# Padding the 264-column slots so that every working tile starts at the same 256-byte phase

## The chip, the cores and the metric

The kernel runs on one core of one Trainium2 chip. The metric is the device time of one execution in microseconds (us). The core has five engines that work at the same time: TensorE (PE; its weight loads are listed as PEld), VectorE (DVE), ScalarE (ACT), GpSimd (POOL) and SyncE (SP, which here issues the transfers). They share an on-chip memory of 128 partitions, SBUF; matmul results go to PSUM, eight banks of 128 x 512 float32. An address in SBUF means the same byte offset in each partition.

## The reference

One decoder layer on 1024 tokens of width 1024, in float32: half a feed-forward block, two attention branches side by side, another half feed-forward block, and a gated per-layer input.

```python
def swiglu(h, w_gate, w_up, w_down):
    return (jax.nn.silu(h @ w_gate) * (h @ w_up)) @ w_down

x = x + 0.5 * swiglu(rms_norm(x, ffn1_norm), ffn1_w_gate, ffn1_w_up, ffn1_w_down)   # D_FF = 2816
h = rms_norm(x, mix_norm)
fq, fk, fv, f_logit, sq, sk, sv, g_fox, g_sb = split_columns(h @ w_in)
# 8 + 8 heads of 64: forgetting attention (causal softmax with cumulated log gates)
# and stick-breaking attention (strictly causal)
merged = sigmoid(g_fox) * (y_fox @ w_branch_fox) + sigmoid(g_sb) * (y_sb @ w_branch_sb)
x = x + merged @ w_out
x = x + 0.5 * swiglu(rms_norm(x, ffn2_norm), ffn2_w_gate, ffn2_w_up, ffn2_w_down)
x = x + sigmoid(rms_norm(x, ple_norm) @ w_ple_gate) * (p @ w_ple_proj)
```

## The kernel before

**Precision.** Each float32 operand of a matmul is split into a high part in fp32r and a low part, the rest (`split` at L102: ACT copies at L103, DVE subtracts at L104; for plain weights ACT at L127 and POOL at L137). A product takes three passes: high by high, high by low, low by high.

**Feed-forward.** Gate and up projections go block by block (256 columns of the weight), each 2x2 block product in seven products instead of eight, from sums of blocks. `product` (L460 to L471, the matmul at L469) runs one of the seven: a group of 12 matmuls, three passes over four 128-row pieces, with a 128x128 stationary piece of the weight tile and a 128x512 moving piece of the tokens' tile. The first blocks go the plain way through L424. The down projection (L364) runs the same scheme with tiles `H` on both sides. A hand-written table (`seqn`) sets the order; the weight tile of a group is prepared four groups ahead (`LA = 4`). POOL makes the sums of weight blocks (L437 to L442).

**Where the weight tiles lie.** The pool `sb` has 13 kinds of slots (tags), each with a fixed number of buffers that are used in turn (`BUFS`). In the feed-forward blocks the prepared weight tile goes, after the first twelve, to a fixed cycle of tags:

```python
tag = tags["hl"][k] if k < len(tags["hl"]) else ("WL", "WL", "WL", "Q", "Q", "PT")[k % 6]
```

`WL` has three buffers and `Q` two, so one round of six groups goes through WL slots 0, 1, 2, Q slots 0, 1 and a PT slot. The moving tiles of L469 lie in `H`, `X` and `T`.

**Middle.** The mixing projections run with tokens stationary (`nat_steps`, L696, 256 or 264 columns moving) or weights stationary (`feat_steps`, L704, 512 tokens moving, weights in `WH` and `WL`); attention runs scores (L935, L936, moving tiles `KH` and `KL`), transposes (L987) and the product with the values (L1009), and the L704 work that is left is put between these in small pieces. The branch projections are L1210 (stationary `WH`, `WL`, moving `H`), the last stage L1477 (stationary `H`, moving `WH`, `WL`, `T`, `GF`, `RN`, `PT`). L854 is the projection of the per-layer input, L224 transposes.

**Slots.** A slot of a tag is as large as the largest tile that the tag ever holds. Three kinds hold tiles of 4 x 264 columns in the mixing projections (the 8 forget logits ride along with 256 columns): `WH`, `WL` and `Y`, so their slots have 4224 bytes, 16.5 times 256. All others are multiples of 256. Tiles lie one behind the other in each partition in the order of first use: X, PT, H, T, WH, KH, KL, WL, Y, Q, GF, RN, RAW. `slot` (L56) asks the pool for a tile, and everything named above is allocated by it.

Of the kernel before, what the change touches and what calls it, by code (L numbers as in the profile page):

```python
# [18 lines left out]
P = 128  # L19
# [10 lines left out]
PSUM = {"sc": 3, "pt": 2, "av": 1, "pf": 2}  # L30
BUFS = {"X": 2, "H": 4, "RAW": 2, "WH": 3, "WL": 3, "T": 4, "GF": 2, "RN": 2,
        "Q": 2, "KH": 2, "KL": 2, "Y": 2, "PT": 3}
FQ, FK, FV, FL, SQ, SK, SV, GFOX, GSB = 0, 512, 1024, 1536, 1544, 2056, 2568, 3080, 4104


@with_exitstack
def tile_hybrid_decoder_layer(
# [6 lines left out]
    nc = tc.nc  # L44
    cp = ctx.enter_context(tc.tile_pool(name="const", bufs=1))
    st = ctx.enter_context(tc.tile_pool(name="stats", bufs=4))
    sb = ctx.enter_context(tc.tile_pool(name="sb", bufs=2))
# [4 lines left out]
    def nm(s):  # L52
        uid[0] += 1
        return f"{s}_{uid[0]}"

    def slot(tag, shape, dt=F32):  # L56
        return sb.tile(shape, dt, tag=tag, bufs=BUFS[tag], name=nm(tag))

    def stat(shape, tag, bufs=4):
        return st.tile(shape, F32, tag=tag, bufs=bufs, name=nm(tag))  # L60
# [51 lines left out]
    def wraw_load(pieces, nk, n, tag="RAW"):  # L112
        raw = slot(tag, [P, nk, n])
        c = 0
        for src in pieces:
            w = src.shape[-1]
            nc.sync.dma_start(raw[:, :, c:c + w], src)
            c += w
        return raw
# [5 lines left out]
    def whigh(raw, nk, n, tag):  # L125
        hi = slot(tag, [P, nk, n], F32R)
        order("wh", nc.scalar.copy(hi[:], raw[:]))  # L127
        return hi

    def wlow(raw, hi, nk, n, tag, eng_lo=nc.gpsimd):  # L130
        lo = slot(tag, [P, nk, n], F32R)
        if nk == 1:
            parts = [(slice(None), slice(None), slice(i * n // 2, (i + 1) * n // 2)) for i in range(2)]
        else:
            parts = [(slice(None), slice(i * nk // 2, (i + 1) * nk // 2)) for i in range(2)]
        for part in parts:
            ins = eng_lo.tensor_sub(lo[part], raw[part], f(hi[part]))  # L137
            if eng_lo is nc.gpsimd:
                order("wl", ins)
        return lo  # L140
# [900 lines left out]
    def mix_start():  # L1041

        mx["v"], mx["qk"] = {}, {}
        mx["u1"] = v_units(FV + 256, NH, mx["v"])
        tags = (("T", "GF"), ("T", "Y"))
        mx["u2"] = fox_qk_units(FOX_PAIRS[0], mx["qk"], tags, "KH")
        q0 = FOX_PAIRS[0] * P
        pieces = [[kp(win)[:, 4 * kh:4 * kh + 4, a:a + n] for a, n in cols] for cols in (((FV + 256, 256 + NH),), ((FQ + q0, P), (FK + q0, P))) for kh in range(2)]
        raws = {}

        def load_v(X):
            raws["v"] = [wraw_load(pieces[kh], 4, 256 + NH, "Y") for kh in range(2)]

        def split_v(X):
            mx["v"]["w"] = [wsplit(raws["v"][kh], 4, 256 + NH, NAT[kh]) for kh in range(2)]

        def load_qk(X):
            raws["qk"] = [wraw_load(pieces[2 + kh], 4, 256) for kh in range(2)]

        def end(X, N):  # L1060
            hT.extend(halves(N))
            store_x(X, 1)
            for cell in loads[:2]:
                cell[1] = None
            side = posts(N[1], (24, 64, 104, 144), lambda: bank("pt"))
            side[48] = [lambda: mx["qk"].update(w=[wsplit(raws["qk"][kh], 4, 256, tags[kh]) for kh in range(2)])]
            weave(seq(*[g for _, g in mx["u1"][:4] + mx["u2"][:4]]), side)
        return {3: [load_v], 4: [split_v], 5: [lambda X: store_x(X, 0)], 6: [load_qk], "end": end}
# [164 lines left out]
    X = [slot("X", [P, 4, D]) for _ in range(2)]  # L1233
# [86 lines left out]
    X, N = ffn(N, ffn1_w_gate, ffn1_w_up, ffn1_w_down, mix_norm[0], x[0], ad[0], tags, first_entry, mix_start())  # L1320
# [178 lines left out]
    X, hT = [], []  # L1499
# [34 lines left out]
```

## Time and profile before

| What | Value |
|---|---|
| runs | 2302.49, 2301.84, 2300.70 us; median 2301.84 |
| the profiled execution, first to last instruction (span) | 2300.6 us |
| busy PE / DVE / ACT / POOL | 2269.6 / 1468.0 / 980.7 / 829.9 us |
| PE clock granted, mean | 0.999 |
| moved by DMA | 275.49 MB, mean 120 GB/s |
| first feed-forward: products, then down | about 60 to 450, then 450 to 655 us |
| mixing, attention, branches, output | about 655 to 1580 us |
| second feed-forward: products, then down | about 1580 to 1990, then 1990 to 2195 us |
| last stage | about 2195 to 2300 us |

The profiled execution's own time is known as its span; the median of the three runs stands 1.2 us above it. In the rows below, `ps<-H,WL` names the tiles of an instruction without their numbers, `x1008` is how many there are, and `L469` the line of the kernel before. Matmuls overlap in the pipeline, so the mean length of one (some 390 ns) is more than the distance from one start to the next.

### The profile page before, as it was taken

The numbers are of one execution on the slowest core, as the hardware profiler recorded it, in microseconds if no ns is written. First come the engines' busy times: TensorE is split into PE (matmuls) and PEld (weight loads), VectorE is DVE, ScalarE is ACT, GpSimd is POOL, SyncE is SP. The second block draws the span as 40 slices with busy tenths as digits, with TensorE's granted clock in tenths as the row PEclk, the third lists the DMA queues.
The fourth block names the chain that finished last, engine by engine and source line by source line (L and its number), as shares of the span: only waits on it lengthen the run. The fifth ranks groups of instructions, "written<-read, shape, count | busy, mean of one in ns | idle before, by whom it ended". The sixth has DMA issues, their size and how long they took to land.

```text
span 2300.6 us, 30661 instructions
## 1 busy us (share of the span) xinstructions
PE 2269.6 (99%) x11466; PEld 1913.6 (83%) x11466; DVE 1468.0 (64%) x2199; ACT 980.7 (43%) x1742; POOL 829.9 (36%) x762
## 2 busy tenths in 40 slices
PE   9999999999999999899999999999999999999999
PEld 6888888888888999798988778888888888888887
DVE  8855555588863566456656766789645454778753
ACT  6433333333442555555555554246333333334431
POOL 2344444300033556545455645400534343200111
PEclk9999999999999999999999999999999999999999
DMA  3232323484332122422133235732423232655232
GB/s 138 92 124 83 124 83 123 142 307 168 103 120 75 52 79 74 137 79 71 50 82 89 74 115 199 258 139 74 138 78 128 78 128 78 226 213 205 70 106 92
DMA packets 188279, 275.49 MB, mean 120 GB/s; under 512 B 27097, under 2 KB 110297, under 8 KB 188130
## 3 DMA queue, kind: packets, MB, share of 16 engines
q1 hardware_dynamic: 188128, 273.53, 35.4%
q8 instruction: 90, 1.47, 0.3%
q14 instruction: 59, 0.48, 0.1%
q10 hardware_dynamic: 2, 0.00, 0.0%
HBM read 189.83 MB, written 75.27 MB: 115 GB/s over the span
## 4 chain that ended last, share of the span: by engine, by line
PE 55%; DVE 2%; ACT 1%; issue 0%; DVEq 0%; ACTq 0%
PE ps L469 18%; PE ps L364 12%; PE ps L704 9%; PE ps L1477 4%; PE ps L1210 4%; PE ps L1009 2%; PE ps L696 2%; PE ps L987 2%; DVE RN L911 1%; PE ps L424 1%; PE ps L936 1%; PE ps L935 1%; PE ps L854 1%; PE ps L224 0%; DVE H L104 0%
## 5 line engine op out<-in xcount | busy, mean ns | idle before, releaser
L364 PE MATMUL ps<-H,H 128*128 128x512 f32 x2184 | 497.8, 389 | 1.2 <-DVE X L372 1.2
L364 PEld LDWEIGHTS ps<-H,H 128*128 128x128 f32 x2184 | 409.3, 188 | 86.8 <-issue 2.0
L469 PE MATMUL ps<-H,WL 128*128 128x512 f32 x1008 | 244.6, 394 | 0.6 <-ACT WL L103 0.6
L469 PEld LDWEIGHTS ps<-H,WL 128*128 128x128 f32 x1008 | 189.7, 188 | 44.7 <-ACT WL L103 1.0
L704 PE MATMUL ps<-H,WH 128*128 128x512 f32 x768 | 209.5, 401 | 2.1 <-DVE PT L819 2.1
L137 POOL TENSOR_TENSOR WL<-RAW,WH 128x512 fp32r<-128x512 f32 (+1 forms) x108 | 129.4, 1219 | 101.2 <-ACT WH L127 72.9
L704 PEld LDWEIGHTS ps<-H,WH 128*128 128x128 f32 x768 | 136.8, 188 | 26.3 <-DVE PT L819 3.0
L990 DVE TENSOR_TENSOR PT<-ps,PT 128x512 fp32r<-128x512 f32 (+1 forms) x160 | 101.2, 633 | 84.4 <-ACT PT L989 83.6
L137 POOL TENSOR_TENSOR WL<-Y,WH 128x512 fp32r<-128x512 f32 (+1 forms) x10 | 14.4, 1465 | 383.1 <-ACT WH L127 383.1
L469 PE MATMUL ps<-H,Q 128*128 128x512 f32 x600 | 143.9, 390 | 0.0
L372 DVE SCALAR_TENSOR_TENSOR X<-ps,X 128x512 f32<-128x512 f32 x168 | 109.0, 685 | 50.9 <-PE ps L364 50.9
L696 PE MATMUL ps<-WH,H 128*128 128x256 f32 (+1 forms) x896 | 131.7, 286 | 2.0 <-ACT RN L753 0.7
L469 PEld LDWEIGHTS ps<-H,Q 128*128 128x128 f32 x600 | 112.6, 188 | 24.5
L989 ACT CAST PT<-ps 128x512 fp32r<-128x512 f32 (+1 forms) x160 | 87.2, 547 | 106.7 <-PE ps L987 102.1
L469 PE MATMUL ps<-X,WL 128*128 128x512 f32 x504 | 123.8, 394 | 0.0
L696 PEld LDWEIGHTS ps<-WH,H 128*128 128x128 f32 x896 | 116.5, 189 | 4.1 <-ACT RN L753 0.9
L469 PEld LDWEIGHTS ps<-X,WL 128*128 128x128 f32 x504 | 94.9, 188 | 22.0
L1009 PE MATMUL ps<-PT,X 128*128 128x256 f32 (+1 forms) x640 | 104.4, 283 | 8.8 <-DVE PT L990 8.8
L1009 PEld LDWEIGHTS ps<-PT,X 128*128 128x128 f32 x640 | 94.7, 190 | 21.0 <-DVE PT L990 11.0
L704 PE MATMUL ps<-H,WL 128*128 128x512 f32 x384 | 108.6, 404 | 0.0
L948 POOL TENSOR_TENSOR T<-T,l 128x128 f32<-128x128 f32 (+3 forms) x64 | 73.3, 1149 | 89.6 <-DVE l L947 87.2
L911 DVE TENSOR_TENSOR_SCAN RN<-GF,RN 128x127 f32<-128x127 f32 (+2 forms) x96 | 102.2, 1065 | 2.7
(400 smaller groups left out, 4680.0 us busy)
## 6 DMA issues: line engine op xcount, KB each, us to landing
hidden<-PT SPq DMA_DIRECT2D x40, 512.0 KB, 3.1
WH<-in_ffn_w_gate_dram SPq DMA_DIRECT2D x38, 512.0 KB, 5.0
Q<-hidden SPq DMA_DIRECT2D x24, 512.0 KB, 6.4
hidden<-RN SPq DMA_DIRECT2D x22, 512.0 KB, 2.6
RAW<-in_w_in_dram SPq DMA_DIRECT2D x22, 512.0 KB, 4.1
KH<-in_ffn_w_up_dram SPq DMA_DIRECT2D x20, 512.0 KB, 5.8
KL<-in_ffn_w_up_dram SPq DMA_DIRECT2D x20, 512.0 KB, 6.6
T<-in_ffn_w_down_dram SPq DMA_DIRECT2D x20, 512.0 KB, 4.4
```

The costliest lines, as they stand in the source:

```text
L137: ins = eng_lo.tensor_sub(lo[part], raw[part], f(hi[part]))
L364: pe(nc.tensor.matmul(groups[g][t][:], act[:, a, k, t * P:(t + 1) * P], wt[:, b, k, :], start=(fresh and n == 0), stop=(i in (6, 1, 4) and ...
L372: nc.vector.scalar_tensor_tensor(xs, groups[g][t][:], scale, xs, ALU.mult, ALU.add)
L469: pe(nc.tensor.matmul(ps[:], hl[:, a, k, :], rhs(m, b, k), start=(first and i == 0), stop=(final and i == 11), skip_group_check=True))
L696: pe(nc.tensor.matmul(ps[:, :n], hT[t // 4][a][:, k, (t % 4) * P:(t % 4 + 1) * P], w[k // 4][b][:, k % 4, :n], start=(i == 0), stop=(i == ...
L704: pe(nc.tensor.matmul(ps[:], w[a][:, k, :], hT[half][b][:, k, :], start=(i == 0), stop=(i == 23)))
L911: order("dve", nc.vector.tensor_tensor_scan(*args))
L989: high = nc.scalar.copy(pt[:, 0, :width], ps[:, :width])
L990: low = nc.vector.tensor_sub(pt[:, 1, :width], ps[:, :width], f(pt[:, 0, :width]))
L1009: pe(nc.tensor.matmul(o, lh, r, start=(kpair == c and i == 0), stop=(kpair == 0 and i == 3)))
L1210: pe(nc.tensor.matmul(ps[:], w[a][:, k, :], yT[g][b][:, k, half * 512:half * 512 + 512], start=(i == 0), stop=(i == 11)))
L1477: pe(nc.tensor.matmul(ps, hT[t // 4][a][:, k, (t % 4) * P:(t % 4 + 1) * P], pl["w"][d, k // 2][b][:, k % 2, cs], start=(i == 0), stop=(i = ...
```

## The change

It alters only where tiles lie in SBUF. `slot` now asks for a flat tile of a fixed size per tag (`SIZE`, in float32 elements) and hands out a view of it with the old shape; WH, WL and Y get 1088 elements, 4352 bytes, in place of 4224, and RAW gets 4352 in place of 4096. The room for it comes from the descriptor area at the bottom of SBUF, which goes from 16384 to 8192 bytes, so that everything above it moves down.

```diff
+SIZE = {"X": 4096, "H": 4096, "RAW": 1088, "WH": 1088, "WL": 1088, "T": 1024, "GF": 1024, "RN": 1024,
+        "Q": 1024, "KH": 1024, "KL": 1024, "Y": 1088, "PT": 1024}
...
     def slot(tag, shape, dt=F32):
-        return sb.tile(shape, dt, tag=tag, bufs=BUFS[tag], name=nm(tag))
+        n = 1
+        for d in shape[1:]:
+            n *= d
+        t = sb.tile([P, SIZE[tag]], dt, tag=tag, bufs=BUFS[tag], name=nm(tag))[0:shape[0], 0:n]
+        if len(shape) == 2:
+            return t
+        names = "abcd"[:len(shape) - 1]
+        return t.rearrange(f"p ({' '.join(names)}) -> p {' '.join(names)}", **dict(zip(names, shape[1:])))
...
-    nc = _bacc.Bacc("TRN2", target_bir_lowering=False, num_devices=1)
+    nc = _bacc.Bacc("TRN2", target_bir_lowering=False, num_devices=1, dynamic_dma_scratch_size=8192)
```

Start addresses in the built programs, per slot, and their phase (address modulo 256):

| Tag | before: addresses | phase | after: phase |
|---|---|---|---|
| X | 19328, 35712 | 128, 128 | 128 |
| PT | 52096, 56192, 60288 | 128, 128, 128 | 128 |
| H | 64384, 80768, 97152, 113536 | 128 each | 128 |
| T | 129920, 134016, 138112, 142208 | 128 each | 128 |
| WH | 146304, 150528, 154752 | 128, 0, 128 | 128 |
| KH | 158976, 163072 | 0, 0 | 128 |
| KL | 167168, 171264 | 0, 0 | 128 |
| WL | 175360, 179584, 183808 | 0, 128, 0 | 128 |
| Y | 188032, 192256 | 128, 0 | 128 |
| Q | 196480, 200576 | 128, 128 | 128 |
| GF | 204672, 208768 | 128, 128 | 128 |
| RN | 212864, 216960 | 128, 128 | 128 |
| RAW | 221056, 225152 | 128, 128 | 128 |

After the change X begins at 11136 and RAW ends at 222592. The 128-row pieces that a matmul reads lie 512 bytes apart inside a tile of the feed-forward blocks, so they have the phase of their tile. The instructions, their order on each engine and their waits are the same in both programs.

## The prediction

> **What bounds the kernel now.** I read the page first: how busy each engine is, and at which clock.
>
> ```profile
> span 2300.6 us, 30661 instructions
> PE 2269.6 (99%) x11466; PEld 1913.6 (83%) x11466; DVE 1468.0 (64%) x2199; ACT 980.7 (43%) x1742; POOL 829.9 (36%) x762
> PEclk9999999999999999999999999999999999999999
> ```
>
> PE works in 99% of the span at a full granted clock, no other engine in more than 64%. So PE's idle time is not the place to look; the time from one matmul's start to the next one's is. The chain in order of time gives that, where it runs unbroken through one line (columns: start, length, count; all in us):
>
> ```profile
> 1417.57 60.77 PE ps L1210 x264
> 1478.35 70.72 PE ps L364 x312
> 1579.74 11.09 PE ps L424 x48
> 1590.83 399.92 PE ps L469 x1740
> 1990.75 125.16 PE ps L364 x552
> ```
>
> All of these are 128x128 by 128x512 matmuls of the same type. L364 (the down projection) takes 125.16/552 = 226.7 ns each, and again 70.72/312 = 226.7. L469 (the seven products) takes 399.92/1740 = 229.8 ns, L1210 230.2 and L424 231.0. PE waits for nobody there, and yet 3 to 4 ns are lost per matmul. The groups by tile names say with which tiles (out<-moving,stationary in any order; after the bar the busy us and the mean ns of one, whose length includes what a matmul is held up):
>
> ```profile
> L364 PE MATMUL ps<-H,H 128*128 128x512 f32 x2184 | 497.8, 389 | 1.2 <-DVE X L372 1.2
> L469 PE MATMUL ps<-H,WL 128*128 128x512 f32 x1008 | 244.6, 394 | 0.6 <-ACT WL L103 0.6
> L704 PE MATMUL ps<-H,WH 128*128 128x512 f32 x768 | 209.5, 401 | 2.1 <-DVE PT L819 2.1
> L469 PE MATMUL ps<-H,Q 128*128 128x512 f32 x600 | 143.9, 390 | 0.0
> L469 PE MATMUL ps<-X,WL 128*128 128x512 f32 x504 | 123.8, 394 | 0.0
> L704 PE MATMUL ps<-H,WL 128*128 128x512 f32 x384 | 108.6, 404 | 0.0
> L469 PE MATMUL ps<-H,PT 128*128 128x512 f32 x408 | 97.7, 390 | 0.0
> L1210 PE MATMUL ps<-H,WH 128*128 128x512 f32 x256 | 81.1, 394 | 0.0
> L469 PE MATMUL ps<-T,WL 128*128 128x512 f32 x240 | 58.9, 394 | 0.0
> L1210 PE MATMUL ps<-H,WL 128*128 128x512 f32 x128 | 50.9, 397 | 0.0
> L1477 PE MATMUL ps<-WH,H 128*128 128x512 f32 x92 | 26.4, 396 | 0.1
> L854 PE MATMUL ps<-WH,X 128*128 128x512 f32 x64 | 19.3, 408 | 3.1 <-ACT PT L860 1.2 <-DVE KL L778 1.1 <-DVE X L104 0.4
> L935 PE MATMUL ps<-KH,Q 128*128 128x512 f32 x48 | 19.1, 397 | 1.3 <-ACT T L944 1.3
> ```
>
> H, X, T, PT and Q lie at phase 128 in all their slots, and give 389 to 390. WL, WH, KH and KL have slots at phase 0, and give 394 and more, on the stationary side (L469) and on the moving side (L1477, L935) alike. One round of six groups shows the single slots, because their tags follow a fixed order: PT, WL slot 0 (phase 0), WL slot 1 (128), WL slot 2 (0), Q slot 0 (128), Q slot 1 (128), and PT again. PE timeline, start and length in us:
>
> ```profile
> 313.31 2.89 PE L469 MATMUL ps<-X,PT 128*128 128x512 f32 x12
> 316.04 2.96 PE L469 MATMUL ps<-H,WL 128*128 128x512 f32 x12
> 318.83 2.92 PE L469 MATMUL ps<-T,WL 128*128 128x512 f32 x12
> 321.59 2.96 PE L469 MATMUL ps<-H,WL 128*128 128x512 f32 x12
> 324.39 2.91 PE L469 MATMUL ps<-H,Q 128*128 128x512 f32 x12
> 327.14 2.88 PE L469 MATMUL ps<-X,Q 128*128 128x512 f32 x12
> 329.86 0.39 PE L469 MATMUL ps<-H,PT 128*128 128x512 f32 x1
> ```
>
> From start to start: 2.73, 2.79, 2.76, 2.80, 2.75, 2.72 us. Twelve matmuls of L364 would take 2.72. So the group whose stationary tile is at phase 0 loses 0.07 to 0.08 us, the group just behind it, though all its tiles are at 128, still loses 0.03 to 0.04, and the next one, Q slot 1, loses nothing. It is not the tile's name (WL slot 1 and WL slots 0 and 2 differ), but the two phases that do not match, with an after-effect that dies out within one group.
>
> **The change part by part.** Both programs have the same instructions in the same order on every engine, with the same waits; only SBUF addresses differ. So nothing is added or moved in a queue, and I cost three things.
>
> *Matching phases on PE.* All stationary and moving tiles of the working pool now start at 128, which is the state of L364. What each line can win, in matmuls times the loss per matmul:
>
> - L469: 1008+504+240 with WL, 600+336+168 with Q, 408+168+96 with PT, together 3528, by 229.84-226.74 = 3.10 ns: 10.9 us. A second way: 16.55 us a round against 6 x 2.72 = 16.32, 0.23 us by 3528/72 = 49 rounds: 11.3. I take 10.9.
> - L1210: 384 by 230.2-226.7 = 3.5 ns is 1.3 us; a little of it is the wait at the head of some groups, so 1.1.
> - L424: 192 by 231.0-226.7 = 4.3 ns is 0.8; some groups wait for their splits, so 0.6.
> - L1477: 92 with WH by 396-389 ns: 0.6. Its other groups I leave out.
> - L704: at most 768 x 12 + 384 x 15 ns = 15 us, at least nothing. Its matmuls run singly and in pairs between other shapes in attention, and most of its surplus is such a hand-over, since lines with no phase 0 at all show it too (L1009's 128x256 below is one of them). Nearest is L1210, the same weights in whole groups with 3.5 ns: a quarter of that on 1152 matmuls, 1.0 us. Both ends stay for the range.
> - L854 and L935, and L936 beside it, which read WH, KH and KL: 0.3 together, between nothing and 64 x 19 ns + 48 x 8 ns = 1.6.
>
> Sum 10.9+1.1+0.6+0.6+1.0+0.3 = 14.5 us of PE time. L696's 128x256 and 128x264 matmuls I cost at nothing: their mean is about the same for tiles of either kind.
>
> ```profile
> L696 PE MATMUL ps<-WH,H 128*128 128x256 f32 x768 | 114.7, 286 | 1.9 <-ACT RN L753 0.7 <-ACT PT L860 0.6 <-DVE X L104 0.5
> L696 PE MATMUL ps<-T,H 128*128 128x256 f32 x128 | 17.0, 284 | 0.9 <-DVE log_f L735 0.9
> L1009 PE MATMUL ps<-PT,X 128*128 128x256 f32 x512 | 102.8, 291 | 4.8 <-DVE PT L990 4.8
> ```
>
> What of this reaches the end? In the first feed-forward block PE is the only engine near its limit (stretch, its length, then busy us and count of PE, weight loads, DVE, ACT, POOL, then PE's clock, DMA share and GB/s):
>
> ```profile
> 60.00:450.00 390.00, 390.00 (x1698) 318.96 (x1697) 216.11 (x258) 136.70 (x238) 160.80 (x113) 1.00 0.31 108
> ```
>
> DVE has 174 us to spare there, so 5 us less of PE leaves it covered. The waits of PE that exist (L1009 for DVE 4.8, L854 3.1) stay as they are. I count the whole 14.5.
>
> *Elementwise engines.* They read and write the same tiles at another phase. Two lines that do the same work on tiles of either phase:
>
> ```profile
> L437 POOL TENSOR_TENSOR RAW<-KH 128x512 f32<-128x512 f32 x19 | 24.5, 1290 | 0.0
> L437 POOL TENSOR_TENSOR RAW<-WH 128x512 f32<-128x512 f32 x17 | 22.0, 1296 | 62.2 <-DMA WH<-in_ffn_w_gate_dram 62.2
> L778 DVE SCALAR_TENSOR_TENSOR KL<-ps,gqk,KH 64x512 fp32r<-64x512 f32 x16 | 12.1, 757 | 0.4
> L777 DVE SCALAR_TENSOR_TENSOR Q<-ps,gqk,Q 64x512 fp32r<-64x512 f32 x16 | 11.9, 745 | 7.9 <-ACT KH L776 7.5
> ```
>
> KH at phase 0 costs POOL 1290 ns, WH (two slots in three at 128) 1296; on DVE phase 0 is 12 ns dearer. Between -12 and +6 ns on work that PE covers: nothing.
>
> *Transfers and the descriptor area.* KH, KL and some slots of WH, WL and Y go from phase 0 to 128. Rows with the same source and size (median us to landing last), and the page's row of SP's queue:
>
> ```profile
> GF<-hidden SPq DMA_DIRECT2D x14, 512.0 KB, 8.6
> KH<-hidden SPq DMA_DIRECT2D x14, 512.0 KB, 8.3
> KL<-hidden SPq DMA_DIRECT2D x8, 512.0 KB, 9.1
> q1 hardware_dynamic: 188128, 273.53, 35.4%
> ```
>
> GF (128) takes 8.6, KH and KL (0) 8.3 and 9.1: between -0.5 and +0.3 us with no sign to it, so nothing. All but 2 MB of the 275.49 MB that the page counts go through q1, which SP feeds; no row shows the descriptor area in use, and its halving costs nothing.
>
> The sum goes against the profiled execution: 2300.6-14.5 = 2286.1. The median of the runs, 2301.84, stands 1.2 us above that span, so I forecast 2301.84-14.5 = 2287.3 us.
>
> **The rivals.**
>
> *Nothing changes.* The 5 ns could belong to how WL and WH are produced. Against it: WL slot 1 has the same producers as slots 0 and 2, and KH on the moving side (397) is produced in another way. Time: 2301.8, within 0.2%, which is about what a measurement here can tell from no change. [...] 4%.
>
> *Slower, by the transfers.* If pieces that begin off a 256-byte boundary were dearer, the weight loads into KH and KL (20 pairs) and WH would land later. The place is the first product of a pair of weight blocks: POOL already waits 62.2/17 = 3.7 us for such loads. Stationary tiles are prepared four groups ahead, 4 x 2.75 = 11 us; less that wait and three POOL sums of 1.3 us some 3 us are left, and only beyond that does PE wait. With 0.8 us (KH to KL above) past that point on each of the 44 weight blocks of both layers it would be +35-14.5 us, 2322. [...] 3%.
>
> *Half of it.* A faster PE meets its suppliers, above all in attention, or tiles at one common phase leave some loss that L364 hides by its regular order: 7 us, 2294.6. DVE's spare time speaks against it. 9%.
>
> *More.* L704's surplus is phase after all: 5 to 10 us on top, 2277 to 2282. Its interleaving speaks against it. 6%.
>
> **How the numbers follow.** The forecast, 2287.3, has 78%, with 2284 to 2292 as its own range. I widen it to 2282 to 2294, which takes in most of the half case and the edge of "more". Faster holds forecast, half and more, 93%; same 4%; slower 3%.
>
> **What would show it.** In the changed profile L469's rows with WL should read 389 to 390 like those with PT; a round of six groups should take 16.3 us; L469's chain of 1740 should take 394.5 us; L364 must stay at 226.7 a matmul; L1210 should come near 227, L704 move by a few ns. KH and KL loads should land as before. I am wrong if WL rows stay at 394, if L364 rises (then the common phase itself costs), or if PE shows new idle time in L469 behind DMA or ACT.

## The result, and the profile after

The changed kernel takes 2289.8 us, the median of four runs (2286.81 to 2291.45), beside 2302.16 us of the kernel before on the same chip (four runs, 2300.70 to 2302.63). The ratio is 0.9945, with a 95% interval from 0.9931 to 0.9959: faster by 12.4 us, 0.55%, where 14.5 us was forecast. The profiled execution has a span of 2287.2 us, 13.4 us less than the one before.

The page says who became shorter. PE's busy time falls by 14.8 us (from 2269.6 to 2254.8), that of the others by less than 2 us, and the number of instructions is the same.

```profile
span 2287.2 us, 30661 instructions
PE 2254.8 (99%) x11466; PEld 1913.9 (84%) x11466; DVE 1467.6 (64%) x2199; ACT 980.1 (43%) x1742; POOL 828.1 (36%) x762
```

All lines of the kernel have moved down by 9: L469 is now L478, L364 is L373, L1210 is L1219, L424 is L433, L704 is L713, L1477 is L1486. The chain in order of time (start, length, count) holds the same pieces as before:

```profile
1411.46 59.87 PE ps L1219 x264
1471.33 70.72 PE ps L373 x312
1572.54 10.88 PE ps L433 x48
1583.42 394.40 PE ps L478 x1740
1977.82 125.13 PE ps L373 x552
...
2213.84 69.28 PE ps L1486 x328
```

L478 takes 394.40/1740 = 226.7 ns a matmul instead of 229.8, L1219 59.87/264 = 226.8 instead of 230.2, L433 10.88/48 = 226.7 instead of 231.0. L373, whose tiles had matched before, stays at 226.7. In the groups by tile names, L478's rows with WL have come down from 394 to 389, where L373 stands. L713, whose matmuls run between other shapes, keeps its means of 401 and 404, and L863 even rose (L713, L863, L944 are L704, L854, L935; why L863 rose is told below):

```profile
L373 PE MATMUL ps<-H,H 128*128 128x512 f32 x2184 | 497.8, 389 | 1.2 <-DVE X L381 1.2
L478 PE MATMUL ps<-H,WL 128*128 128x512 f32 x1008 | 239.4, 389 | 0.8 <-ACT WL L112 0.8
L713 PE MATMUL ps<-H,WH 128*128 128x512 f32 x768 | 209.2, 401 | 2.0 <-DVE PT L828 2.0
L478 PE MATMUL ps<-H,Q 128*128 128x512 f32 x600 | 143.1, 389 | 0.0
...
L713 PE MATMUL ps<-H,WL 128*128 128x512 f32 x384 | 108.6, 404 | 0.0
...
L1219 PE MATMUL ps<-H,WH 128*128 128x512 f32 x256 | 80.5, 392 | 0.0
...
L863 PE MATMUL ps<-WH,X 128*128 128x512 f32 x64 | 20.3, 426 | 2.6 <-ACT PT L869 1.2 <-DVE KL L787 1.1 <-DVE PT L828 0.3
L944 PE MATMUL ps<-KH,Q 128*128 128x512 f32 x48 | 18.9, 394 | 1.3 <-ACT T L953 1.3
```

One round of six groups in PE's timeline (start and length): every group now starts 2.72 us after the one before it, 16.32 us for the round, where 2.72 to 2.80 had alternated.

```profile
310.17 2.88 PE L478 MATMUL ps<-H,WL 128*128 128x512 f32 x12
...
315.61 2.88 PE L478 MATMUL ps<-H,WL 128*128 128x512 f32 x12
318.33 2.88 PE L478 MATMUL ps<-H,Q 128*128 128x512 f32 x12
...
323.77 2.88 PE L478 MATMUL ps<-H,PT 128*128 128x512 f32 x12
```

WL's slots now lie 4352 = 17 x 256 bytes apart, so neighbours differ modulo 512 and still give the same 2.72 us: a match modulo 256 is enough here.

Where along the execution the time went can be read from starts of the same piece of work. The last matmul of the first down projection starts at 663.1 us before and at 655.4 after (-7.7); the chain of L424 ahead of the second block at 1579.74 and 1572.54 (-7.2); the last chain of L1477 at 2226.93 and 2213.84 (-13.1); the end is at 2300.6 and 2287.2 (-13.4).

From the kernel before, the two rows that the prediction did not show (the first is line L364 from 440 us on: its shortest, median and longest matmul in ns, first and last start in us):

```profile
L364 PE MATMUL ps<-H,H x924: 387/389/476, 451.2 to 663.1; 128*128 128x512 f32 x185
...
2226.93 69.63 PE ps L1477 x328
```

and the row of the changed kernel that answers to the first:

```profile
L373 PE MATMUL ps<-H,H x924: 387/389/476, 443.4 to 655.4; 128*128 128x512 f32 x185
```

By these marks the middle (mixing, attention, branches, output) would have lost 0.5 us, but two things in them have nothing to do with the change. The first is the start. The execution before began its work later (last section): already the first group of L469, at the beginning of the first block, starts at 50.50 us before and at 47.96 us after.

The second is the clock. In the middle of both profiled executions there are stretches of 3.4 us in which PE was granted half its clock, and they fall differently in the two. Two windows of the kernel before (start and end, length, then busy us and count of PE, weight loads, DVE, ACT, POOL, then PE's clock, DMA share and GB/s):

```profile
935.00:960.00 25.00, 21.13 (x110) 16.89 (x111) 10.29 (x29) 10.70 (x21) 8.54 (x10) 1.00 0.53 146
1350.00:1375.00 25.00, 20.39 (x105) 16.76 (x104) 18.55 (x23) 13.10 (x28) 15.28 (x17) 0.93 0.53 168
```

and two of the changed kernel:

```profile
935.00:960.00 25.00, 20.05 (x95) 15.34 (x94) 12.15 (x36) 13.93 (x27) 9.00 (x11) 0.93 0.54 153
1345.00:1365.00 20.00, 16.31 (x75) 13.63 (x76) 14.72 (x20) 9.39 (x21) 11.20 (x13) 0.83 0.64 202
```

A mean of 0.93 over 25 us is one such stretch, 0.83 over 20 us two. The profile before holds one, that of the changed kernel three, and one of them, from 942.7 to 946.1 us, lies on matmuls of L863.

Since PE runs the same 11466 matmuls in the same order in both, the distances from start to start can be set against each other one by one, without the first 30 us, the stretches and the 4 us behind each of them (196 matmuls are left out that way). What is left is 13.0 us: 5.4 up to the end of the first down projection, 1.3 in the middle, 5.9 from there to the last chain, 0.4 after it. The parts left out add 2.3 us at the start and take 1.9 in the stretches. A second profile of the changed kernel, set against the same profile before, gives 12.9 us. So the two feed-forward blocks carry most of the gain, and the middle and the last stage add a little.

### The profile page after: what moved, and what is told of

Its sections match the earlier page's. It is cut to its first block, busy times and chain, and to the rows that moved or that the text cites. A ratio compares the mean times of both kernels' runs of the same rounds, so it can differ in the third digit from the quotient of the medians.

```text
span 2287.2 us, 30661 instructions
## 1 busy us (share of the span) xinstructions
PE 2254.8 (99%) x11466; PEld 1913.9 (84%) x11466; DVE 1467.6 (64%) x2199; ACT 980.1 (43%) x1742; POOL 828.1 (36%) x762
## 4 chain that ended last, share of the span: by engine, by line
PE 55%; DVE 2%; ACT 1%; issue 0%; DVEq 0%; ACTq 0%
PE ps L478 17%; PE ps L373 12%; PE ps L713 9%; PE ps L1486 4%; PE ps L1219 4%; PE ps L1018 2%; PE ps L705 2%; PE ps L996 2%; DVE RN L920 1%; PE ps L433 1%; PE ps L945 1%; PE ps L944 1%; PE ps L863 1%; PE ps L233 0%; DVE H L113 0%
## 5 line engine op out<-in xcount | busy, mean ns | idle before, releaser
L373 PE MATMUL ps<-H,H 128*128 128x512 f32 x2184 | 497.8, 389 | 1.2 <-DVE X L381 1.2
L373 PEld LDWEIGHTS ps<-H,H 128*128 128x128 f32 x2184 | 409.4, 188 | 86.7 <-issue 2.0
L478 PE MATMUL ps<-H,WL 128*128 128x512 f32 x1008 | 239.4, 389 | 0.8 <-ACT WL L112 0.8
L478 PEld LDWEIGHTS ps<-H,WL 128*128 128x128 f32 x1008 | 189.1, 188 | 40.4 <-ACT WL L112 1.2
L713 PE MATMUL ps<-H,WH 128*128 128x512 f32 x768 | 209.2, 401 | 2.0 <-DVE PT L828 2.0
L713 PEld LDWEIGHTS ps<-H,WH 128*128 128x128 f32 x768 | 136.9, 188 | 26.1 <-DVE PT L828 3.0
L478 PE MATMUL ps<-H,Q 128*128 128x512 f32 x600 | 143.1, 389 | 0.0
L705 PE MATMUL ps<-WH,H 128*128 128x256 f32 (+1 forms) x896 | 131.9, 287 | 2.0 <-ACT RN L762 0.7
L478 PEld LDWEIGHTS ps<-H,Q 128*128 128x128 f32 x600 | 112.6, 188 | 23.4
L478 PE MATMUL ps<-X,WL 128*128 128x512 f32 x504 | 121.1, 389 | 0.0
L705 PEld LDWEIGHTS ps<-WH,H 128*128 128x128 f32 x896 | 116.9, 190 | 4.0 <-ACT RN L762 0.9
L478 PEld LDWEIGHTS ps<-X,WL 128*128 128x128 f32 x504 | 94.6, 188 | 19.6
L713 PE MATMUL ps<-H,WL 128*128 128x512 f32 x384 | 108.6, 404 | 0.0
L957 POOL TENSOR_TENSOR T<-T,l 128x128 f32<-128x128 f32 (+3 forms) x64 | 73.2, 1148 | 90.9 <-DVE l L956 88.5
```

Of the source, the lines that this page charges most:

```text
L373: pe(nc.tensor.matmul(groups[g][t][:], act[:, a, k, t * P:(t + 1) * P], wt[:, b, k, :], start=(fresh and n == 0), stop=(i in (6, 1, 4) and ...
L478: pe(nc.tensor.matmul(ps[:], hl[:, a, k, :], rhs(m, b, k), start=(first and i == 0), stop=(final and i == 11), skip_group_check=True))
L705: pe(nc.tensor.matmul(ps[:, :n], hT[t // 4][a][:, k, (t % 4) * P:(t % 4 + 1) * P], w[k // 4][b][:, k % 4, :n], start=(i == 0), stop=(i == ...
L713: pe(nc.tensor.matmul(ps[:], w[a][:, k, :], hT[half][b][:, k, :], start=(i == 0), stop=(i == 23)))
```

## The experiments

My theory was: a 128x128 by 128x512 matmul takes 226.7 ns if the stationary and the moving tile lie at the same phase (address modulo 256 bytes), and 3 to 5 ns more if they don't. The rivals: the smaller descriptor area or the lower addresses did it; phase 128 itself is what is good; the loss grows with the distance of the phases. All edits below are to the changed kernel except the first, which is to the kernel before. Lines of the edited kernels stand 12 below those of before (L469 is L481, L364 is L376), of the last pad experiment 14 below (L483).

**The descriptor area alone.**

```diff
-    nc = _bacc.Bacc("TRN2", target_bir_lowering=False, num_devices=1)
+    nc = _bacc.Bacc("TRN2", target_bir_lowering=False, num_devices=1, dynamic_dma_scratch_size=8192)
```

> The old slots with only the descriptor area cut to 8192 bytes, so every address moves down by 8192 and every phase stays as before. Theory (two phases that do not match cost PE): nothing changes, 2302 us within 0.2%, the unbroken L469 chain of 1740 matmuls stays at 399.9 us, WL rows at 394 ns. Rival (the smaller area, or the lower addresses, brought the gain): about 2290 us, and the chain at 394.4.

Measured: 2301.33 us (ten runs) beside 2300.74 us (nineteen runs), ratio 0.9999, interval 0.9990 to 1.0008. The chain of L469 has the length that it had before, to the hundredth of a microsecond:

```profile
1591.71 399.92 PE ps L469 x1740
```

So the lower addresses and the halved area do nothing that shows within 0.1%, and the gain is the padding's.

**All tiles at phase 0 instead of 128.** A pad of 128 bytes ahead of the first slot moves every slot.

```diff
+        if tag == 'X' and 'pad' not in ring_pad:
+            ring_pad['pad'] = sb.tile([P, 32], F32, tag='pad', bufs=1, name=nm('pad'))
         t = sb.tile([P, SIZE[tag]], dt, tag=tag, bufs=BUFS[tag], name=nm(tag))[0:shape[0], 0:n]
```

> The changed kernel with 128 bytes put in front of its first working tile, so that every working tile starts at phase 0 instead of 128. Theory (only the match of the phases counts): as the changed kernel, 2290 us within 0.2%, L469 chain 394.4 us, its WL rows and the rows of the down projection at 389 ns. Rival (phase 0 itself is slow, 5 ns for each matmul that reads a tile there): all of the some 7800 matmuls of 512 columns slow down, the down projection too, 394 ns in its rows, about 2290+40 = 2330 us.

Measured: 2289.39 us, ratio to before 0.9946 (0.9931 to 0.9961). The group with WL is that of the changed kernel:

```profile
L481 PE MATMUL ps<-H,WL 128*128 128x512 f32 x1008 | 239.3, 389 | 0.8 <-ACT WL L115 0.8
```

and so is the chain:

```profile
1584.84 394.40 PE ps L481 x1740
```

It is the match that counts; neither 0 nor 128 is better in itself.

**All tiles from WH on at phase 0, the others at 128.** The same pad ahead of the first WH slot. X, PT, H and T stay at 128, and all the rest goes to 0: the slots keep one common phase in each half, but the halves don't match.

```diff
+        if tag == 'WH' and 'pad' not in ring_pad:
+            ring_pad['pad'] = sb.tile([P, 32], F32, tag='pad', bufs=1, name=nm('pad'))
         t = sb.tile([P, SIZE[tag]], dt, tag=tag, bufs=BUFS[tag], name=nm(tag))[0:shape[0], 0:n]
```

> The changed kernel with 128 bytes put ahead of WH, so that X, PT, H and T stay at phase 128 and WH, KH, KL, WL, Y, Q, GF, RN and RAW all lie at 0. Theory (mismatch): in L469 five groups of six (WL and Q) now mismatch at some 5.9 ns a matmul, the PT group has the after-effect: 5 x 12 x 5.9 + 35 = 390 ns a round, 49 rounds, 19 us over the changed kernel, with L1210, L704, L424 and L1477 some 3 us more: 2290+22 = 2312 us, slower than before. The down projection (H with H) stays at 389 ns. Rival (the gain came from something else in the layout than the match): no slower than before, 2302 us or less.

Measured: 2311.09 us, ratio 1.0040 (1.0025 to 1.0055), slower than before, as it should be if five of the six groups of a round are mismatched (three with WL, two with Q) instead of two. The groups:

```profile
L376 PE MATMUL ps<-H,H 128*128 128x512 f32 x2184 | 497.8, 389 | 1.2 <-DVE X L384 1.2
L481 PE MATMUL ps<-H,WL 128*128 128x512 f32 x1008 | 245.3, 395 | 0.5 <-ACT WL L115 0.5
L481 PE MATMUL ps<-H,Q 128*128 128x512 f32 x600 | 146.6, 395 | 0.0
...
L481 PE MATMUL ps<-H,PT 128*128 128x512 f32 x408 | 97.8, 390 | 0.0
```

The chain in order of time:

```profile
1593.69 402.98 PE ps L481 x1740
```

Q, which had 390 before, has 395 once it is at 0; PT, which stayed at 128, keeps 390; H with H stays at 389. No tile's producer was changed for this, so the name of the tile and who wrote it are ruled out. The same 1740 matmuls take 402.98 us here against 394.40 in the changed kernel. That it is PE's reads of the two tiles that hold each other up is my inference and not shown; shown is that the time depends on both addresses together, as moving all tiles to 0 costs nothing and moving one side does.

**Only WL back at its old phases (0, 128, 0).** A pad of 128 bytes ahead of WL and its slots at 4224 bytes again; WH, KH, KL, Y and the rest stay at 128.

```diff
-SIZE = {"X": 4096, "H": 4096, "RAW": 1088, "WH": 1088, "WL": 1088, "T": 1024, "GF": 1024, "RN": 1024,
+SIZE = {"X": 4096, "H": 4096, "RAW": 1088, "WH": 1088, "WL": 1056, "T": 1024, "GF": 1024, "RN": 1024,
...
+        if tag == 'WL' and 'pad' not in ring_pad:
+            ring_pad['pad'] = sb.tile([P, 32], F32, tag='pad', bufs=1, name=nm('pad'))
```

> The changed kernel with WL alone at its old phases 0, 128, 0; all other working tiles at 128. Theory: nearly all of L469's gain goes, chain back to 399.9 us, WL slots 0 and 2 lose 0.07 to 0.08 us a group, and the groups behind them 0.03; L1210 loses half of its gain; total 2290+10.7+0.5 = 2301 us. The groups of Q that follow a WL group at phase 0 show 390 ns in their rows again, though Q has not moved. Rival (the loss lay with the placement of KH, KL, WH and Y too, by transfers or elementwise work): the time stays nearer to 2290, half of the gain or more is kept.

Measured: 2301.9 us (ten runs), ratio 1.0000 (0.9991 to 1.0010). The groups:

```profile
L481 PE MATMUL ps<-H,WL 128*128 128x512 f32 x1008 | 244.7, 394 | 0.6 <-ACT WL L115 0.6
L481 PE MATMUL ps<-H,Q 128*128 128x512 f32 x600 | 143.9, 390 | 0.0
```

The chain in order of time:

```profile
1588.36 399.92 PE ps L481 x1740
```

With WL alone the whole gain is gone again, and the chain is that of before to the hundredth of a microsecond. WH, KH, KL and Y contribute nothing that a comparison of whole executions tells. L1210 lost 0.8 us of the 1.0 that it had gained, where half was expected.

**Other distances.** The pad ahead of WH with 8, 16, 24, 40, 48 or 56 words of 4 bytes in place of 32 puts the second half of the tiles at phase 160, 192, 224, 32, 64 or 96; H, X and T stay at 128. One run each.

```diff
-            ring_pad['pad'] = sb.tile([P, 32], F32, tag='pad', bufs=1, name=nm('pad'))
+            ring_pad['pad'] = sb.tile([P, 8], F32, tag='pad', bufs=1, name=nm('pad'))
```

> As the kernel with the second half of the pool at phase 0, but that half (WH, KH, KL, WL, Y, Q, GF, RN, RAW) at 160, so 32 bytes past the phase 128 of X, PT, H and T. Theory A (each mismatch costs the same): L469's unbroken chain of 1740 matmuls takes 403 us as there, one look near 2310 us. Theory B (the loss grows with the distance between the two phases): a quarter of the 8.6 us of that chain, 396.5 us, near 2294.

> The same with 64 bytes between the two phases (192 against 128). Theory A: chain 403 us. Theory B: half of the loss, 398.7 us. [...]

> The same with 96 bytes between the two phases (224 against 128). Theory A: chain 403 us. Theory B: three quarters of the loss, 400.8 us. [...]

> The same with the second half at phase 64, 64 bytes before the 128 of the others. If only the distance counts, the chain is that of +64 bytes; if the sign counts (which stream runs ahead), it differs from that by more than 1 us.

The last two were chosen after these four:

> The second half of the pool (WH to RAW) at phase 96, 32 bytes before the 128 of X, PT, H and T. Shown so far for L469's chain of 1740: 394.4 us at distance 0, 397.6 at -64, 403.0 at 128, 404 to 405 at +32, +64 and +96. If the loss grows evenly on the negative side, -32 takes 396 us, near 2294 in one look. If a small lead of the weight load helps, the chain falls below 394.4.

> The same at phase 32, 96 bytes before the others. Even growth on the negative side gives 400 us for the chain (between 397.6 at -64 and 403.0 at 128). If every distance but a few costs the full 5 to 6 ns, 403 to 405.

Measured, with the two earlier kernels in their places (distance is the phase of the stationary tile less that of the moving one):

| Distance, bytes | chain of 1740, us | ns a matmul | WL group, mean ns | whole execution, us |
|---|---|---|---|---|
| -96 | 405.09 | 232.8 | 395 | 2314.96 |
| -64 | 397.57 | 228.5 | 391 | 2296.54 |
| -32 | 403.92 | 232.1 | 395 | 2310.88 |
| 0 (the changed kernel) | 394.40 | 226.7 | 389 | 2289.8 |
| +32 | 404.09 | 232.2 | 395 | 2313.12 |
| +64 | 404.59 | 232.5 | 396 | 2311.22 |
| +96 | 405.21 | 232.9 | 396 | 2320.31 |
| 128 | 402.98 | 231.6 | 395 | 2311.09 |

The chain at distance -64:

```profile
1586.46 397.57 PE ps L481 x1740
```

and at +64:

```profile
1594.35 404.59 PE ps L481 x1740
```

The chain is the column to compare: the whole executions are single runs, and their granted clocks differ (a mean of 0.997 at +96 and of 0.999 at +64).

The theory that the cost grows with the distance falls: 32 bytes off costs as much as 128. So does the hope that some distance is better than a match: nothing is below 394.40. Nearly every mismatch costs the full 5 to 6 ns on average over the chain, of which five groups in six are mismatched, but not all: at -64 it is less than 2 ns, and +64 has the full price. Which of the two is ahead matters, then, not only by how much. Both readings that I had put down for -32 (even growth to 396 us, or below the match) were wrong; of the two for -96, even growth failed and the full cost came. The mechanism by which the two addresses cost time, and why -64 is let off, stay open.

**WH alone at the cheap distance.** In these runs one group moved the other way. L696's 1344 matmuls with 256 moving columns (L708 here) add up, from start to start, to 165.3 us before, 165.8 in the changed kernel, and 162.3 at -64, 163.7 at +64 and +32. (In L696 the tiles of the second half are the moving ones, so the sign of the distance is the other way round there.) So I put WH alone at phase 64, to see whether the kernel could keep L469's gain and win 2 us there, and ran the changed kernel beside it once more.

```diff
+        if tag == 'WH' and 'WH' not in pads:
+            pads['WH'] = sb.tile([P, 48], F32, tag='pad_' + tag, bufs=1, name=nm('pad'))
+        if tag == 'KH' and 'KH' not in pads:
+            pads['KH'] = sb.tile([P, 16], F32, tag='pad_' + tag, bufs=1, name=nm('pad'))
```

> The changed kernel with WH alone at phase 64, all else at 128. In the kernel with the whole second half at 64 the 128x256 matmuls of the mixing projections, with WH and WL moving, took 162.3 us in sum in place of 165.8, while L469, L1210 and L1477 lost. WH is moving in 896 of these 1344. Theory (the sign that helps a weight load hurts or helps a moving tile on its own): -2.3 us there, +0.3 in L1210, +0.2 in L704, +0.5 in L1477, so 1 us faster than the changed kernel, 2288 to 2289. Rival (a mixture of phases costs in the after-effect as in the kernel before): 1 to 3 us slower than the changed kernel.

> The changed kernel once more, beside the one with WH at 64 and the kernel before. 2289 to 2290 us, 12 us less than before. Of the profiled span: the start should be either about 3 us quicker or not, as the clock goes to full 4 or 13 us after the first instruction; the L469 chain 394.4 us in either case.

Measured: 2289.34 us (2287.57 to 2289.44) with WH at 64, 2287.87 us (2287.18 to 2291.37) for the changed kernel; ratios to before 0.9951 (0.9936 to 0.9966) and 0.9950 (0.9933 to 0.9967). The 256-column matmuls did become shorter. With WH at 64, the group and the last chain are:

```profile
L710 PE MATMUL ps<-WH,H 128*128 128x256 f32 x768 | 113.5, 285 | 1.9 <-ACT RN L767 0.7 <-ACT PT L874 0.6 <-DVE X L118 0.5
...
2213.59 70.06 PE ps L1491 x328
```

and in the changed kernel beside it:

```profile
L705 PE MATMUL ps<-WH,H 128*128 128x256 f32 x768 | 115.1, 287 | 1.9 <-ACT RN L762 0.7 <-ACT PT L869 0.6 <-DVE X L113 0.5
...
2213.25 69.28 PE ps L1486 x328
```

By sums of start to start L705's line gains 1.7 us, L1219 and L1486, whose WH is now mismatched, lose 0.6 and 1.0. That cancels, and the times can't tell the two kernels apart: neither the gain of 1 us nor the loss of 1 to 3 us that were put down for WH at 64 is decided. In its profile the changed kernel has the earlier start again (last section). No version beat the changed kernel measurably.

## Why the prediction was right, and where it was not

The forecast was 2287.3 us; 2289.8 us was measured, within the range. The mechanism was the one that was argued. The terms came out as follows; "whole" is the sum of the distances from start to start over the whole execution (before, less after), and "outside" the same without the start and the half-clock stretches:

| Term of the sum | forecast, us | whole, us | outside, us |
|---|---|---|---|
| L469, matching phases | 10.9 | 10.7 (811.6 to 800.9) | 10.7 |
| L1210 | 1.1 | 1.0 (89.5 to 88.5) | 1.0 |
| L1477 | 0.6 | 0.5 (82.7 to 82.2) | 0.5 |
| L424 | 0.6 | 0.2 (46.1 to 45.9) | 0.6 |
| L704 | 1.0 | 0.4 (276.4 to 276.0) | 0.8 |
| L854, L935, L936 | 0.3 | -0.5 on L854 (28.1 to 28.6) | 0.2 |
| L696, costed at nothing | 0 | -0.5 (165.3 to 165.8) | -0.5 |
| L1009, costed at nothing | 0 | -0.7 (87.1 to 87.8) | -0.5 |

*L469* carried nearly everything, and its price was right because the trace of before held both cases side by side, in one line with the same producers. The tests that were named came out: WL rows at 389, a round of 16.32 us, a chain of 394.40 us where 394.5 was forecast, L364 unchanged, L1210 at 226.8 ns.

*L1210 and L1477* were right for the same reason.

*L424, L704 and L854* look sized too high by the sums over the whole execution, and their rows after the change still show 399 (L433 with H and WL, the first groups of each block), 401 and 404 (L713) and 426 (L863). That is where a sum over one profile misleads. Part of L424 runs in the first 30 us, and in the changed kernel's earlier start it waits 0.7 us more; a stretch at half clock lies on L863 in the changed kernel and on no L854 before; on L704 lie one stretch before and two after. In the second profile of the changed kernel, L704's whole sum is 274.4, a gain of 2.0 instead of 0.4, while outside it is again 0.8. Outside, the three terms are 0.6, 0.8 and 0.2 where 0.6, 1.0 and 0.3 were forecast. The rest of L704's surplus over 389 is still there with all tiles matching, so it is not phase, as the prediction had argued when it counted only a small part of it.

*L696 and L1009* are where the sum was too high. L696 was taken as neutral because its means were alike for tiles of either kind; it lost 0.5 us. The runs at other distances show that the phase matters there too, with the other sign: of the seven mismatched kernels of the table six have a sum of L696 below the 165.8 of the match, by 0.4 to 3.5 us, and +96 has 0.5 more. Why is open. L1009, which has all its tiles at 128 in both kernels, lost 0.5 us as well (0.4 and 0.5 with all tiles at 0 and in the second profile of the changed kernel); it runs between L704's matmuls, and what makes it longer is open. These two, and L469 and L704 by 0.2 us each, make most of the difference between 14.5 and the 13.0 us outside. The measured 12.4 us have an interval of 9.4 to 15.9 (0.41 to 0.69% of 2302), in which both lie, so the times of whole executions alone could not have told these sizes.

*Elementwise engines* were right in effect. POOL's sum from KH went from 1290 to 1294 ns, DVE's L778 from 757 to 756, inside the bounds (so the 12 ns between L777 and L778 were not phase); POOL's sum from WH went from 1296 to 1318 ns, beyond the upper bound of 6 ns, but PE covers it.

*Transfers* were a step that did not hold. It said that the loads would land as before, because the rows for `hidden` had no sign to their difference. The weight loads of 256 columns, with pieces of 1024 bytes, do have one. DMA issues of the kernel before (count, KB, median us from issue to landing):

```profile
WH<-in_ffn_w_gate_dram SPq DMA_DIRECT2D x38, 512.0 KB, 5.0
KH<-in_ffn_w_up_dram SPq DMA_DIRECT2D x20, 512.0 KB, 5.8
KL<-in_ffn_w_up_dram SPq DMA_DIRECT2D x20, 512.0 KB, 6.6
```

of the changed kernel:

```profile
WH<-in_ffn_w_gate_dram SPq DMA_DIRECT2D x38, 512.0 KB, 5.5
KH<-in_ffn_w_up_dram SPq DMA_DIRECT2D x20, 512.0 KB, 6.3
KL<-in_ffn_w_up_dram SPq DMA_DIRECT2D x20, 512.0 KB, 6.9
```

and with all tiles at phase 0:

```profile
WH<-in_ffn_w_gate_dram SPq DMA_DIRECT2D x38, 512.0 KB, 5.0
KH<-in_ffn_w_up_dram SPq DMA_DIRECT2D x20, 512.0 KB, 5.9
KL<-in_ffn_w_up_dram SPq DMA_DIRECT2D x20, 512.0 KB, 6.5
```

In the changed kernel they land 0.3 to 0.5 us later, 5 to 10% of the time to landing, with all tiles at phase 0 they don't. For KH and KL this holds in nine profiles: 5.8 to 5.9 and 6.4 to 6.6 us where both lie at phase 0 (the kernel before, the descriptor area alone, all tiles at 0, all from WH on at 0), 6.2 to 6.3 and 6.9 to 7.0 where they lie at another (the changed kernel twice, WL at its old phases, -64, WH alone at 64). What makes them later is not shown: in the kernel before, the 27 WH loads that went to a slot at 128 landed after 4.9 us and the 11 that went to the slot at 0 after 5.2 (medians), so a load's own phase does not explain WH. The consequence that the rival "slower by the transfers" drew did not come. POOL waits for those loads 64.3 us instead of 62.2:

```profile
L446 POOL TENSOR_TENSOR RAW<-WH 128x512 f32<-128x512 f32 x17 | 22.4, 1318 | 64.3 <-DMA WH<-in_ffn_w_gate_dram 64.3
```

which is 0.12 us a load, less than the some 3 us that were left before PE would notice. PE's only wait on WL in L478 is 0.8 us in all. With all tiles aligned at 0 and matched, the loads are as quick as before, and the execution, 2289.39 us, is no shorter: the step had the wrong size and no weight.

The rival "nothing changes" falls by the edits that moved the second half of the tiles and WL alone. "Half of it" and "more" fall with L469's 10.7 us and L704's 0.8.

## What to carry to other kernels

Where matmuls run back to back at full rate, look at the time from one start to the next, not at PE's idle time: a surplus of a few ns that was different for tiles of the same shape and type (394 ns beside 389) pointed here to where the tiles lie. Here giving the stationary and the moving tiles the same address modulo 256 was worth 3 to 6 ns of 230 in a matmul of 512 columns. A slot size that is no multiple of 256 puts the slots behind it at other phases than the tiles they work with, so it is worth a look at the addresses in the built program. Price such an effect from two rows that differ in it alone; in a row whose mean is made up of hand-overs, count only a part by the nearest clean row. When two profiles are compared for half a microsecond, look first where the clock was at half in each (3.4 us here, once before and three times in the changed kernel), and compare the same matmuls outside these places.

## What the runs showed that was not expected

*The price has no grade, and one exception.* A distance of 32 bytes costs as much as 128 (404.09 and 402.98 us beside 394.40), but -64 bytes costs a third of +64 (397.57 and 404.59 us).

*An after-effect.* A group whose tiles match took 0.03 to 0.04 us longer when it stood behind one that doesn't: 2.76 us for WL slot 1 and 2.75 for Q slot 0 in the round shown ahead of the prediction's sum. Where the group ahead matches, as in all of the changed kernel's round, it is 2.72 us.

*Two ways to start.* In some executions the matmuls of the first 12 us run at half rate, in others only the first few of them, whatever the kernel. PE's timeline of the kernel before:

```profile
4.80 3.78 PE L189 MATMUL ps<-PT,T 1*128 1x512 f32 x4
...
50.50 1.75 PE L469 MATMUL ps<-H,PT 128*128 128x512 f32 x7
```

of the changed kernel (L189 is L198):

```profile
4.45 1.98 PE L198 MATMUL ps<-PT,T 1*128 1x512 f32 x4
...
47.96 4.24 PE L478 MATMUL ps<-H,PT 128*128 128x512 f32 x18
```

and of the kernel with all tiles at phase 0, which has the padding and begins like the kernel before:

```profile
4.80 3.78 PE L201 MATMUL ps<-PT,T 1*128 1x512 f32 x4
```

The same four matmuls take 3.78 us or 1.98. The records of PE's clock in the traces begin, at full, 13.6 us after the first instruction in the kernel before and 4.0 us after it in the changed kernel. In the changed kernel the first group of L469 at the beginning of the first block starts 2.5 us earlier. Some 0.5 us of that belongs to the change: the kernel with all tiles at 0 begins as slowly as the kernel before, and starts that group 0.5 us earlier. The kernel before and the one with all tiles at 0 began with 3.78, the changed kernel both times with 1.98, and in the kernel with WL alone at its old phases, which is no faster than before, the groups of the first block stand 2.4 us earlier than before too (the X group with PT starts at 310.88 us beside 313.31). The nineteen runs of the kernel before in one series fall in two groups, ten from 2300.31 to 2300.74 us and nine from 2302.03 to 2303.05, with none between. The start, or one half-clock stretch more (3.4 us at half clock, so up to 1.7 us lost), would each fit their distance; neither was shown. A difference between two single profiles of up to 2.5 us is therefore no finding here unless the same instructions are compared outside these places.
